# Memory and retention values projected 512 columns at a time, one token chunk to a PSUM bank

## The chip, the cores and the metric

The kernel runs on one core of a Trainium2 chip. The metric is the device time of one execution in microseconds (us), lower is better. The kernel before took 964.93 us (median of 3 runs, 964.29 to 968.08).

## What is computed

Two layers of a decoder trunk on 512 tokens of width 1024. Each layer normalizes the tokens, projects them with one combined matrix, runs four mixers on the parts, gates each, maps them back and adds the residual. Cut to the parts that matter here:

```python
hn = rmsnorm(x, pre_g)                       # (512, 1024)
proj = hn @ w_in                             # ret_q, ret_k, ret_v, ..., sb_q, sb_k, sb_v, mem_q, ...
k, v = split(rmsnorm(mem, mem_norm_g) @ w_mem_kv, 2)   # 256 memory tokens, k and v (256, 512)
y_mem = softmax(mem_q @ k.T * d**-0.5) @ v   # 4 heads of 128
y_sb  = stick_breaking(sb_q, sb_k, sb_v)     # 4 heads of 128, strictly causal
y_ret = retention(rope(ret_q), rope(ret_k), ret_v)     # 4 heads of 128, then a norm per head
y_ssd = ssd_mixer(xbc, z, dt, ...)
x = x + rmsnorm(concat(gated y's) @ w_out, post_g)
```

The values of the memory (256 tokens by 512 columns) and of the retention (512 tokens by 512 columns) are what the change touches.

## The kernel before

**Precision and matmuls.** Every operand is kept as a pair of tiles, a high part and a low part, and every product is three matmuls: high by high, high by low, low by high (`mm3`). The helper `mm` at L278 issues nearly all of them, so their rows all carry that line and are told apart by tiles: `pj` and `mx` are PSUM banks (a bank is 128 partitions by 512 float32), `hTh` and `hTl` the transposed normed tokens, `wh` and `wl` the weights, `s` and `y` working tiles. In the profile's names for a matmul, `pj<-wh,hTh` has the operand that streams first and the stationary one second.

**Weights.** They come from HBM in blocks of 1 MB (`raw`). Each block is two pieces of 128 x 1024, and each piece is split into `wh` (a cast on ACT, L286) and `wl` (a subtraction on DVE, L287). There are 5 buffers for pieces (`NSUB`) and 2 for blocks. A piece's buffer is free again when the last matmul that reads it is done, and only then can a later piece be split into it. For an "a" block a piece holds four 128-row chunks of the width by 256 columns.

**Projections with the tokens stationary.** `proj_a` computes 256 output columns for up to 4 token chunks of 128: two chunks share one PSUM bank, a piece is used for all chunks, and then the next piece follows. One call takes 2 pieces and 96 matmuls of 256 columns for 4 chunks, 48 for 2. `proj_b` has the weights stationary and 512 tokens streaming: one piece and 24 matmuls of 512 columns for 128 output features.

**PSUM.** There are two pools of 4 banks, `pj` and `mx`. A new bank can be taken when one of the four in its pool has been read for the last time.

**The order of the work.** In the first part of layer 0 (`start`) the instructions stand as written. After that a scheduler places the instructions of each engine at build time, and `tick` and `defer` decide after how many projections a later step of a head is issued. Each engine then works through its own fixed list, in that order, and waits where an operand or a bank is not ready.

**The stretch that matters here.** In a layer the stick-breaking heads run before the retention. Head h projects its query and its key (`proj_b` twice, into two `pj` banks). The query is read out by L531 (ACT) and L532 (DVE), the key by L286 (ACT) and L287 (DVE, `s<-pj`). Then follow, for each of four token blocks of 128, 256, 384 and 512 keys: the logits in an `mx` bank, an absolute value, an exponential and a logarithm on ACT (L619 and L255), then on DVE a maximum (L622), a running sum (L623) and a difference (L625), then an exponential (L255). `sb_head2` transposes the weights (L637) and splits them (L286 and L287, `s<-mx`), `sb_head3` multiplies them with the values into an `mx` bank. Those last steps of heads 2 and 3 are placed by the scheduler into the retention's value projection (`ret_v`) and the retention's first projections. `ret_v` itself calls `proj_a` twice (half 0 and half 1 of the columns, two banks each), reads each bank with a sum (L657), scales the sum (L658), and subtracts and scales it by four instructions, one for each chunk and head (L662), which is the last reading of the bank. Then it splits the result. `ret_head` goes on with `proj_b` for the query of retention head 0.

Of the kernel before, what the change touches and what calls it, by code (L numbers as in the profile page):

```python
# [16 lines left out]
P = 128  # L17
# [61 lines left out]
def pack_weights(w_in, w_mem_kv, w_out):  # L79
# [3 lines left out]
    for l in range(DEPTH):  # L83
        for kind, name, spec in BLOCKS:
            w = src[name][l]
            o = []
            for s in range(2):
                if kind == "b":
                    t = w[:, spec[s]:spec[s] + P].reshape(KC, P, P)
                elif kind == "o":  # L90
                    half, j = spec
                    rows = OUT_ROWS[4 * j + 2 * s:4 * j + 2 * s + 2]
                    t = np.stack([w[r:r + P, 512 * half:512 * half + 512] for r in rows])
                elif kind == "d":
# [73 lines left out]
class Builder:  # L168
# [196 lines left out]
    def proj_a(self, x=None, nt=NT, extra=0, between=(), turns=False):  # L365
# [154 lines left out]
    def mem_v2(self, b):  # L520
        nc, p = self.nc, Pair(self, 512, "y")
        for t in range(2):
            s, r = slice(256 * t, 256 * t + 256), self.mcol[:, t:t + 1]
            nc.scalar.activation(p.h[:, s], b[:, s], AF.Copy, scale=r)
            nc.vector.scalar_tensor_tensor(out=p.l[:, s], in0=b[:, s], scalar=r, in1=p.hf[:, s], op0=ALU.mult, op1=ALU.subtract)
        self.mv.append(p)


    def scaled_pair(self, b, scale):
# [49 lines left out]
    def mem_head3(self, h, pT, y):  # L579
        b = self.mx()  # L580
        for m in range(2):
            o = 256 * m + HD * (h % 2)
            v = self.mv[h // 2]
# [65 lines left out]
    def ret_v(self):  # L649

        nc = self.nc
        ginv = self.con("ginv", 16)
        out = [[None, None], [None, None]]
        for half in range(2):
            for i, b in enumerate(self.proj_a()):
                st = self.tiny(4)
                nc.vector.tensor_reduce(out=st, in_=v3(b, 4), op=ALU.add, axis=AX.X)  # L657
                nc.vector.tensor_scalar(out=st, in0=st, scalar1=-1.0 / HD, scalar2=None, op0=ALU.mult)  # L658
                vt = self.buf()
                for j in range(4):  # L660
                    t, h = 2 * i + j // 2, 2 * half + j % 2
                    nc.vector.tensor_scalar(out=vt[:, P * j:P * j + P], in0=b[:, P * j:P * j + P],  # L662
                                            scalar1=st[:, j:j + 1], scalar2=ginv[:, 4 * t + h:4 * t + h + 1],
                                            op0=ALU.add, op1=ALU.mult)
                out[i][half] = self.pair(vt)
        return out

    def rope(self, b):
# [42 lines left out]
    def ret_head2(self, h, v, sc, y):  # L711
        nc = self.nc
        b = self.mx()
        for c in range(NT):
            self.mm3(b[:, P * c:], *self.vcols(v, c, h), sc[c][0], sc[c][1], c == 0, c == NT - 1)
        nc.scalar.copy(y, b)
        sq = [self.buf(tag="r")[0:64] for _ in range(2)]
        for i in range(2):
# [227 lines left out]
    def out_proj(self, l):  # L946
# [51 lines left out]
        if not last:  # L998
            for i in range(2):
                self.mem_k2(self.mem_k(i))  # L1000
                self.behind(self.turn[i], self.last_mm)
            for i in range(2):
                self.mem_v()
            self.behind(self.turn[2], self.marks[1])

    def load_x(self, t):
        x = [self.buf(), self.buf()]
# [40 lines left out]
    def start(self):  # L1048
# [33 lines left out]
        hn.append(self.normed(xs[2], preB))  # L1082
        self.w_prefetch(6)
        self.w_load(4)
        v = [self.proj_a(self.mx_, 2, between=[lambda: self.turned(hn[1], 1)])[0]]
        hn.append(self.normed(xs[3], preB))
        self.w_prefetch(7)
        self.mem_add()
        v.append(self.proj_a(self.mx_, 2, between=[lambda: self.turned(hn[2], 2), self.mem_cols])[0])
        self.mem_row()  # L1090
        self.w_load(5)
        self.w_prefetch(10)
        self.turned(hn[3], 3)
        for i in range(2):
            self.mem_v2(v[i])
        self.w_prefetch(12)
        for i in range(2):
            self.mem_k2(k[i])
# [4 lines left out]

    def layer(self, l):
        self.exp_ln_phase()
        while len(self.mv) < 2:
            self.mem_v()
# [54 lines left out]
```

## Time and profile before

| | us |
|---|---|
| median of 3 runs | 964.93 (964.29 to 968.08) |
| the profiled execution | 965.41 |
| its span, first to last instruction | 963.5 |
| PE busy | 950.5 |
| DVE busy | 656.7 |
| ACT busy | 456.7 |
| POOL busy | 101.2 |

The granted TensorE clock was 0.999. Times in the rows are microseconds from the start of the span. Matmuls are pipelined and a matmul's shown duration includes its way through the array, so the pace of PE is read from the distance between the starts of neighbouring matmuls, and not from the duration of one. `[0.24 <-DVE s L532]` behind a row says that the engine stood idle for 0.24 us before it, and that this ended with the DVE instruction of line 532 that wrote a tile `s`.

### The profile page before, as it was taken

The numbers are of one execution on the slowest core, as the hardware profiler recorded it, in microseconds if no ns is written. First come the engines' busy times: TensorE is split into PE (matmuls) and PEld (weight loads), VectorE is DVE, ScalarE is ACT, GpSimd is POOL, SyncE is SP. The second block draws the span as 40 slices with busy tenths as digits, with TensorE's granted clock in tenths as the row PEclk, the third lists the DMA queues.
The fourth block names the chain that finished last, engine by engine and source line by source line (L and its number), as shares of the span: only waits on it lengthen the run. The fifth ranks groups of instructions, "written<-read, shape, count | busy, mean of one in ns | idle before, by whom it ended". The sixth has DMA issues, their size and how long they took to land.

```text
span 963.5 us, 13242 instructions
## 1 busy us (share of the span) xinstructions
PE 950.5 (99%) x5151; PEld 812.5 (84%) x5151; DVE 656.7 (68%) x1054; ACT 456.7 (47%) x842; POOL 101.2 (10%) x160
## 2 busy tenths in 40 slices
PE   8999999999999999999999999999999999999997
PEld 7998888988887878888899888898888878888886
DVE  5765567877877796864487464768776867867454
ACT  6543466534454343553455345765334543435341
POOL 1100000001231201100040000000002321102001
PEclk9999999999999999999999999999999999999999
DMA  9352212122232424253255221212123423323502
GB/s 344 113 176 88 88 45 79 53 88 88 66 132 99 142 103 129 86 188 142 90 185 193 93 88 53 80 45 88 60 79 95 140 99 121 108 101 121 189 30 87
DMA packets 26302, 105.79 MB, mean 110 GB/s; under 512 B 4096, under 2 KB 4352, under 8 KB 16896
## 3 DMA queue, kind: packets, MB, share of 16 engines
q10 hardware_dynamic: 10224, 73.44, 21.5%
q1 hardware_dynamic: 16016, 31.52, 10.0%
q8 instruction: 40, 0.66, 0.3%
q14 instruction: 22, 0.18, 0.1%
HBM read 100.63 MB, written 4.28 MB: 109 GB/s over the span
## 4 chain that ended last, share of the span: by engine, by line
PE 84%; DVE 6%; DMA 5%; ACT 2%; issue 1%; POOL 1%; SPq 0%; DVEq 0%; POOLq 0%; ACTq 0%
PE pj L278 61%; PE mx L278 21%; DMA s<-acs 1%; DVE wl L287 1%; DVE s L623 1%; DMA r<-row 1%; DVE s L786 1%; DMA raw<-wts 1%; PE mx L575 1%; DMA t<-r 1%; POOL t L687 1%; DMA mem<-memT 1%; PE mx L422 0%; DVE s L622 0%; ACT wh L286 0%
## 5 line engine op out<-in xcount | busy, mean ns | idle before, releaser
L278 PE MATMUL pj<-hTh,wh 128*128 128x512 f32 x704 | 277.6, 394 | 0.0
L278 PE MATMUL pj<-hTl,wh 128*128 128x512 f32 x704 | 276.6, 393 | 0.0
L278 PE MATMUL pj<-hTh,wl 128*128 128x512 f32 x704 | 275.4, 391 | 0.0
L287 DVE TENSOR_TENSOR wl<-raw,wh 128x1024 fp32r<-128x1024 f32 (+2 forms) x157 | 186.0, 1189 | 116.2 <-ACT wh L286 109.6
L286 ACT CAST wh<-raw 128x1024 fp32r<-128x1024 f32 (+2 forms) x157 | 160.1, 1023 | 180.1 <-PE pj L278 152.0
L278 PEld LDWEIGHTS pj<-hTh,wl 128*128 128x128 f32 x704 | 132.3, 188 | 26.7
L278 PEld LDWEIGHTS pj<-hTh,wh 128*128 128x128 f32 x704 | 132.3, 188 | 26.6 <-issue 0.2
L278 PEld LDWEIGHTS pj<-hTl,wh 128*128 128x128 f32 x704 | 132.4, 188 | 25.7
L278 PE MATMUL pj<-wh,s 128*128 128x512 f32 (+1 forms) x384 | 103.6, 355 | 0.0
L278 PE MATMUL mx<-s,s 128*128 128x256 f32 (+4 forms) x616 | 97.7, 310 | 0.3
L278 PEld LDWEIGHTS mx<-s,s 128*128 128x128 f32 (+1 forms) x616 | 84.7, 178 | 13.0 <-issue 3.1
L278 PE MATMUL mx<-wh,s 128*128 128x512 f32 x256 | 79.1, 389 | 0.0
L278 PEld LDWEIGHTS pj<-wh,s 128*128 128x128 f32 x384 | 68.3, 189 | 10.5
L278 PE MATMUL pj<-wl,s 128*128 128x512 f32 (+1 forms) x192 | 68.3, 356 | 1.4 <-DVE wl L287 1.4
L706 POOL TENSOR_SCALAR_AFFINE_SELECT s<-s 128x128 fp32r<-128x128 f32 x64 | 21.0, 361 | 417.6 <-DVE s L287 417.6
L278 PE MATMUL pj<-wh,hTh 128*128 128x256 f32 (+1 forms) x208 | 60.2, 290 | 0.5 <-DVE s L532 0.5
L287 DVE TENSOR_TENSOR s<-mx,s 128x512 fp32r<-128x512 f32 (+2 forms) x86 | 42.0, 515 | 26.1 <-ACT s L286 25.7
L278 PE MATMUL pj<-wl,hTh 128*128 128x256 f32 (+1 forms) x208 | 59.5, 286 | 0.0
L278 PE MATMUL pj<-wh,hTl 128*128 128x256 f32 (+1 forms) x208 | 58.5, 284 | 0.0
L278 PEld LDWEIGHTS mx<-wh,s 128*128 128x128 f32 x256 | 48.1, 188 | 10.0
L286 ACT CAST s<-mx 128x512 fp32r<-128x512 f32 (+2 forms) x86 | 36.7, 456 | 39.1 <-PE mx L278 23.1
L287 DVE TENSOR_TENSOR s<-y,s 128x512 fp32r<-128x512 f32 x64 | 41.2, 685 | 19.7 <-ACT s L286 14.0
(165 smaller groups left out, 1316.0 us busy)
## 6 DMA issues: line engine op xcount, KB each, us to landing
raw<-wts ACTq DMA_DIRECT2D x69, 1024.0 KB, 4.8
s<-x SPq DMA_DIRECT2D x24, 256.0 KB, 3.8
raw<-wts SPq DMA_DIRECT2D x4, 1024.0 KB, 8.6
s<-acs SPq DMA_DIRECT2D x16, 256.0 KB, 6.3
r<-row SPq DMA_DIRECT2D x12, 256.0 KB, 3.9
s<-acs SPq DMA_DIRECT2D x16, 128.0 KB, 6.3
x<-s SPq DMA_DIRECT2D x8, 256.0 KB, 2.0
out<-s SPq DMA_DIRECT2D x8, 256.0 KB, 2.0
```

The costliest lines, as they stand in the source:

```text
L278: return self.nc.tensor.matmul(out, lhsT, rhs, start=start, stop=stop)
L286: self.nc.scalar.copy(h, src)
L287: self.nc.vector.tensor_sub(l, src, hf)
L575: nc.tensor.transpose(b[:, P * t:P * t + P], w[t // 2][:, o:o + P], self.con("ident", P))
L623: nc.vector.tensor_tensor_scan(out=u[:, ::-1], data0=u[:, ::-1], data1=u[:, ::-1], initial=0.0, op0=ALU.add, op1=ALU.bypass)
L687: nc.gpsimd.tensor_tensor(out=c, in0=c, in1=self.mhalf[:RP], op=ALU.pow)
L706: nc.gpsimd.affine_select(out=d, in_=d, pattern=[[1, P]], compare_op=ALU.is_ge, fill=0.0, base=0, channel_multiplier=-1)
L786: nc.vector.scalar_tensor_tensor(out=acc[:, s:], in0=b[:, :SEQ - s], scalar=tap(3 - s), in1=acc[:, s:], op0=ALU.mult, op1=ALU.add)
```

## The change

Both value projections get 512 columns at once. A weight piece now holds two 128-row chunks of the width by 512 columns, so a projection takes four pieces, and a token chunk has a bank of its own that all four pieces add to. The retention's values fill four `pj` banks in place of two and two; the memory's fill two, one for each of its 256 tokens' chunks. A matmul has 512 columns in place of 256, and there are half as many. The readers follow: `ret_v` reads four banks of one token chunk and four heads each, and `mem_v2` two banks with one instruction for a chunk on ACT and one on DVE. The bytes of the weights and the number of pieces stay.

```diff
-    b += [("a", "w_mem_kv", GW + 256 * i) for i in range(2)]
+    b += [("v", "w_mem_kv", (GW, 512 * i)) for i in range(2)]
...
-    b += [("a", "w_in", RET_V + 256 * i) for i in range(2)]
+    b += [("v", "w_in", (RET_V, 512 * i)) for i in range(2)]
...
+    def proj_v(self, x=None, nt=NT, between={}):
+        self.tick(2)
+        xh, xl = x or self.hk
+        banks = [self.pj() for _ in range(nt)]
+        self.marks = []
+        for s in range(4):
+            if s == 2:
+                self.tick(2)
+            for f in between.get(s, ()):
+                f()
+            if self.starting:
+                self.w_prefetch(self.w_cur + 2)
+            wh, wl = self.w_take(2)
+            for t in range(nt):
+                ts = slice(P * t, P * t + P)
+                for j in range(2):
+                    kc = 2 * s + j
+                    self.mm3(banks[t], xh(kc)[:, ts], xl(kc)[:, ts], wh[:, j], wl[:, j], kc == 0, kc == KC - 1)
+                self.marks.append(self.last_mm)
+            self.w_prefetch()
+        return banks
...
     def mem_v(self):
-        self.mem_v2(self.proj_a(self.mx_, 2)[0])
+        self.mem_v2(self.proj_v(self.mx_, 2))
...
-        out = [[None, None], [None, None]]
-        for half in range(2):
-            for i, b in enumerate(self.proj_a()):
-                st = self.tiny(4)
-                nc.vector.tensor_reduce(out=st, in_=v3(b, 4), op=ALU.add, axis=AX.X)
-                nc.vector.tensor_scalar(out=st, in0=st, scalar1=-1.0 / HD, scalar2=None, op0=ALU.mult)
-                vt = self.buf()
-                for j in range(4):
-                    t, h = 2 * i + j // 2, 2 * half + j % 2
-                    nc.vector.tensor_scalar(out=vt[:, P * j:P * j + P], in0=b[:, P * j:P * j + P],
...
-                out[i][half] = self.pair(vt)
+        out = []
+        for t, b in enumerate(self.proj_v()):
+            st = self.tiny(HEADS)
+            nc.vector.tensor_reduce(out=st, in_=v3(b, HEADS), op=ALU.add, axis=AX.X)
+            nc.vector.tensor_scalar(out=st, in0=st, scalar1=-1.0 / HD, scalar2=None, op0=ALU.mult)
+            vt = self.buf()
+            for h in range(HEADS):
+                c = slice(HD * h, HD * h + HD)
+                nc.vector.tensor_scalar(out=vt[:, c], in0=b[:, c], scalar1=st[:, h:h + 1],
+                                        scalar2=ginv[:, 4 * t + h:4 * t + h + 1], op0=ALU.add, op1=ALU.mult)
+            out.append(self.pair(vt))
```

The scheduler's order changes with it, at three places of which each comes once in a layer. In the changed kernel's rows the lines have other numbers: L647, L648 and L650 are the former L622, L623 and L625; L558 is the former L532; L290 is L287; L681, L682 and L686 are L657, L658 and L662.

**DVE, middle of the value projection, layer 0.** `pj_1858` and `pj_1859` are the two banks of half 0, `pj_1682` and `pj_1731` hold query and key of stick-breaking head 3, `s_1604` belongs to head 2 and `s_1655` to `s_1659` to the transposed weights of head 1. Before:

```order
L622 SCALAR_TENSOR_TENSOR s_1604<-mx_1641,s_1604 128x512
L657 TENSOR_REDUCE t_1966<-pj_1858 128x4
L287 TENSOR_TENSOR s_1655<-mx_1660,s_1654 128x512
L623 SCALAR_TENSOR_TENSOR s_1604<-s_1604 128x512
L658 TENSOR_SCALAR t_1966<-t_1966 128x4
L287 TENSOR_TENSOR s_1657<-mx_1667,s_1656 128x384
L287 TENSOR_TENSOR s_1659<-mx_1673,s_1658 128x256
L532 SCALAR_TENSOR_TENSOR s_1714<-pj_1682,s_1713 128x512
L625 TENSOR_TENSOR s_1604<-mx_1641,s_1604 128x512
L657 TENSOR_REDUCE t_1978<-pj_1859 128x4
```

In the changed kernel `pj_1806` and `pj_1807` are the banks of token chunks 0 and 1, and `pj_1630` is the query's of head 3:

```order
L681 TENSOR_REDUCE t_1968<-pj_1806 128x4
L682 TENSOR_SCALAR t_1968<-t_1968 128x4
L681 TENSOR_REDUCE t_1980<-pj_1807 128x4
L647 SCALAR_TENSOR_TENSOR s_1552<-mx_1589,s_1552 128x512
L682 TENSOR_SCALAR t_1980<-t_1980 128x4
L290 TENSOR_TENSOR s_1603<-mx_1608,s_1602 128x512
L648 SCALAR_TENSOR_TENSOR s_1552<-s_1552 128x512
L290 TENSOR_TENSOR s_1605<-mx_1615,s_1604 128x384
L290 TENSOR_TENSOR s_1607<-mx_1621,s_1606 128x256
L650 TENSOR_TENSOR s_1552<-mx_1589,s_1552 128x512
L558 SCALAR_TENSOR_TENSOR s_1662<-pj_1630,s_1661 128x512
```

Both sums over the finished banks, and the difference for head 2, now stand ahead of the reading of head 3's query; before, one sum did.

**DVE, end of the value projection, layer 0.** Before, the first bank's last reading (L662 on `pj_1858`) stands ahead of the difference for head 3 (`s_1766`, 512 keys):

```order
L658 TENSOR_SCALAR t_2140<-t_2140 128x4
L623 SCALAR_TENSOR_TENSOR s_1766<-s_1766 128x512
L287 TENSOR_TENSOR s_1821<-mx_1835,s_1820 128x256
L662 TENSOR_SCALAR s_1969<-pj_1858,t_1966,consts 128x128 x4
L625 TENSOR_TENSOR s_1766<-mx_1803,s_1766 128x512
```

In the changed kernel the first bank's last reading (L686 on `pj_1806`) stands behind that difference (`s_1714`) and behind the splits of head 3's transposed weights (`s_1869` to `s_1873`):

```order
L290 TENSOR_TENSOR s_1767<-mx_1788,s_1766 128x128
L650 TENSOR_TENSOR s_1714<-mx_1751,s_1714 128x512
L290 TENSOR_TENSOR s_1869<-mx_1874,s_1868 128x512
L290 TENSOR_TENSOR s_1871<-mx_1881,s_1870 128x384
L290 TENSOR_TENSOR s_1871<-mx_1892,s_1870 128x128
L290 TENSOR_TENSOR s_1873<-mx_1887,s_1872 128x256
L686 TENSOR_SCALAR s_1971<-pj_1806,t_1968,consts 128x128 x4
```

The release of the first of the four value banks has moved past all the remaining work of head 3.

**PE, around the first matmul of the retention's query, layer 0.** Before, `pj_2164` is the query of retention head 0 and `mx_1996` the first transposes of head 3's weights:

```order
L278 MATMUL mx_1844<-s_1820,s_881 128x256
L278 MATMUL mx_1844<-s_1818,s_880 128x128
L637 MATMUL mx_1996<-consts,s_1764 128x128 x2
L637 MATMUL mx_1996<-consts,s_1765 128x128
L278 MATMUL pj_2164<-hTh,wh_1756 128x512
```

In the changed kernel `pj_2016` is that query, and `mx_1896` is the product of head 3's weights with the values, the last step of the stick-breaking heads:

```order
L281 MATMUL mx_1896<-s_1870,s_828 128x128
L281 MATMUL mx_1896<-s_1871,s_828 128x128
L281 MATMUL mx_1896<-s_1870,s_829 128x128
L281 MATMUL pj_2016<-hTh,wh_1704 128x512
L281 MATMUL pj_2016<-hTl,wh_1704 128x512
```

The rest of head 3, which stood among the matmuls of the retention's query and key, now stands ahead of them. Within the value projection PE takes chunk 0 and then chunk 1 through all four weight pieces, then head 3's first logits, then chunks 2 and 3.

More of the change, by code (lines that the diff above doesn't have):

```diff
@@ L93, in pack_weights @@
                     t = np.stack([w[r:r + P, 512 * half:512 * half + 512] for r in rows])
+                elif kind == "v":
+                    rows = slice(spec[1] + 256 * s, spec[1] + 256 * s + 256)
+                    t = w[rows, spec[0]:spec[0] + 512].reshape(2, P, 512)
                 elif kind == "d":
@@ L517, in mem_v, with mem_v2 @@
     def mem_v(self):
-        self.mem_v2(self.proj_a(self.mx_, 2)[0])
[L520 to L526, printed above, removed]
+        self.mem_v2(self.proj_v(self.mx_, 2))
+    def mem_v2(self, banks):
+        nc = self.nc
+        for t, b in enumerate(banks):
+            p, r = Pair(self, 512, "y"), self.mcol[:, t:t + 1]
+            nc.scalar.activation(p.h, b, AF.Copy, scale=r)
+            nc.vector.scalar_tensor_tensor(out=p.l, in0=b, scalar=r, in1=p.hf, op0=ALU.mult, op1=ALU.subtract)
+            self.mv.append(p)
     def scaled_pair(self, b, scale):
@@ L1001, in out_proj @@
                 self.behind(self.turn[i], self.last_mm)
-            for i in range(2):
-                self.mem_v()
-            self.behind(self.turn[2], self.marks[1])
+            self.mem_v()
+            self.behind(self.turn[2], self.marks[5])
     def load_x(self, t):
@@ L1084, in start, with v2 @@
         self.w_load(4)
[L1085 to L1089, printed above, removed]
+        def v2():
+            hn.append(self.normed(xs[3], preB))
+            self.w_prefetch(7)
+            self.mem_add()
+        v = self.proj_v(self.mx_, 2, between={1: [lambda: self.turned(hn[1], 1)], 2: [v2],
+                                             3: [lambda: self.turned(hn[2], 2), self.mem_cols]})
         self.mem_row()
@@ L1093, in start @@
         self.turned(hn[3], 3)
-        for i in range(2):
-            self.mem_v2(v[i])
+        self.mem_v2(v)
         self.w_prefetch(12)
```

10 lines of the change are left out of this document (3 added, 7 removed).

## The prediction

> **What bounds the kernel now.** I read the page's first rows, then the chain of work that ended last.
>
> ```profile
> span 963.5 us, 13242 instructions
> PE 950.5 (99%) x5151; PEld 812.5 (84%) x5151; DVE 656.7 (68%) x1054; ACT 456.7 (47%) x842; POOL 101.2 (10%) x160
> PE 84%; DVE 6%; DMA 5%; ACT 2%; issue 1%; POOL 1%; SPq 0%; DVEq 0%; POOLq 0%; ACTq 0%
> ```
>
> PE is busy almost throughout, and the chain lies on it for 84%. So a shorter list of matmuls shortens the run, if PE still finds work at each moment. That second half has to be read from the stretch of `ret_v`, by the busy time of each engine in it and by its first row on PE's timeline:
>
> ```profile
> 152.90:187.41 34.51, 34.40 (x272) 32.88 (x273) 25.55 (x49) 22.00 (x51) 0.00 (x0) 1.00 0.18 62
> 152.90 0.39 PE L278 MATMUL pj<-wh,hTh 128*128 128x256 f32 x1 [0.24 <-DVE s L532]
> ```
>
> The columns are PE, PEld, DVE, ACT, POOL, granted clock, DMA. DVE has 25.55 us of work in 34.51 us. It is the second engine here, and the value projection begins by waiting for it: the first matmul stood 0.24 us until L532 had read a `pj` bank. The clock is 1.00, so no pace below hides a throttle.
>
> **The matmuls, saved.** The pace of both shapes, from neighbouring starts on PE's timeline:
>
> ```profile
> 162.53 0.28 PE L278 MATMUL pj<-wh,hTh 128*128 128x256 f32 x1
> ...
> 163.61 0.29 PE L278 MATMUL pj<-wh,hTh 128*128 128x256 f32 x1
> 193.18 0.39 PE L278 MATMUL pj<-hTh,wh 128*128 128x512 f32 x1
> ...
> 197.03 0.39 PE L278 MATMUL pj<-hTh,wl 128*128 128x512 f32 x1
> ```
>
> Nine steps of 256 columns take 1.08 us, 0.120 each. Seventeen of 512 take 3.85 us, 0.2265 each. Two narrow ones cost 0.240, one wide one 0.2265, so each removed matmul saves 13.5 ns. Per layer 96 go in `ret_v` (192 become 96) and 48 in the memory's values (96 become 48). That is 1.3 us and 0.65 us, over two layers **3.9 us**, if PE never waits instead.
>
> The Trainium skill, "TensorE: Matmul & The Clock Gate", section "Back-to-back issue gap", gives an isolated gap of N/2.4 + 2.5 ns. By it two halves would cost only 2.5 ns more than one whole, and 288 fewer matmuls would save 0.7 us; the forecast would be 3.2 us higher. The trace does not agree (120 and 226.5 ns against 109 and 216), and the measurement decides.
>
> **The middle of `ret_v`, added wait A.** All four `pj` banks are now open at once. Banks 0 and 1 are there at the start, but chunk 2 needs the one that holds the query of stick-breaking head 3, which L532 frees. DVE's and PE's timelines before:
>
> ```profile
> 163.74 0.60 PE L637 MATMUL mx<-consts,s 128*128 128x128 f32 x4
> 164.09 0.36 PE L278 MATMUL pj<-wl,hTh 128*128 128x256 f32 x1
> 168.18 0.27 PE L637 MATMUL mx<-consts,s 128*128 128x128 f32 x1
> 168.56 1.92 PE L278 MATMUL mx<-s,s 128*128 128x512 f32 x10
> 170.32 0.33 PE L278 MATMUL pj<-wh,hTh 128*128 128x256 f32 x1
> 165.58 0.68 DVE L657 TENSOR_REDUCE t<-pj 128x4 f32<-128x512 f32 x1
> 166.18 0.68 DVE L287 TENSOR_TENSOR s<-mx,s 128x512 fp32r<-128x512 f32 x1
> 166.78 1.21 DVE L623 TENSOR_TENSOR_SCAN s<-s 128x512 f32<-128x512 f32 x1
> 167.91 0.14 DVE L658 TENSOR_SCALAR t<-t 128x4 f32<-128x4 f32 x1
> 167.96 0.88 DVE L287 TENSOR_TENSOR s<-mx,s 128x384 fp32r<-128x384 f32 x2
> 168.76 0.68 DVE L532 SCALAR_TENSOR_TENSOR s<-pj,s 128x512 fp32r<-128x512 f32 x1
> 169.36 0.68 DVE L625 TENSOR_TENSOR s<-mx,s 128x512 f32<-128x512 f32 x1
> 169.96 0.68 DVE L657 TENSOR_REDUCE t<-pj 128x4 f32<-128x512 f32 x1
> ```
>
> Distances of starts give what each occupies DVE: 0.60 for a 512-wide step and for the sum, 1.13 for the running sum, 0.05 for L658, 0.80 for the two narrower splits. Before, L532 stood ahead of the second sum, which can only run when PE has finished that bank. In the new order it stands behind it. So from the moment PE ends chunk 1, DVE has: second sum 0.60, L622 0.60, L658 0.05, split 0.60, running sum 1.13, splits 0.80, L625 0.60, L532 0.68, together 5.1 us. PE meanwhile has head 1's ten transposes (four took 0.35, so 0.9) and ten matmuls of its product (168.56 to 170.32, 1.76) and two first logits (0.2), 2.8 us. The product cannot run ahead, since it needs those splits. **Wait A is 5.1 - 2.8 = 2.3 us.** The stretch before had about 0.3 us of this kind (168.18 to 168.56).
>
> Least: if the second sum and L622 are done as PE ends chunk 1 (1.2 us of the list), 1.1. Most: if two more 512-wide steps lie ahead of them, 3.5. I take the sum of the rows.
>
> **The end of `ret_v`, added wait B.** Retention's query needs a fifth `pj` bank, and all four hold values. The first is free after L662. Before, this stood ahead of head 3's last steps; now it stands behind them all. Rows of DVE and ACT with the durations for that list:
>
> ```profile
> 174.15 0.75 ACT L619 ACTIVATE s<-mx 128x128 f32<-128x128 f32 x2 [3.44 <-PE mx L278]
> 175.63 0.73 DVE L622 SCALAR_TENSOR_TENSOR s<-mx,s 128x128 f32<-128x128 f32 x2 [2.99 <-ACT s L255]
> 176.27 1.00 DVE L623 TENSOR_TENSOR_SCAN s<-s 128x128 f32<-128x128 f32 x2
> 177.19 0.60 DVE L625 TENSOR_TENSOR s<-mx,s 128x128 f32<-128x128 f32 x2
> 178.25 0.56 DVE L622 SCALAR_TENSOR_TENSOR s<-mx,s 128x384 f32<-128x384 f32 x1 [0.46 <-ACT s L255]
> 178.84 0.96 DVE L623 TENSOR_TENSOR_SCAN s<-s 128x384 f32<-128x384 f32 x1
> 179.71 1.20 DVE L287 TENSOR_TENSOR wl<-raw,wh 128x1024 fp32r<-128x1024 f32 x1
> 180.83 0.55 DVE L625 TENSOR_TENSOR s<-mx,s 128x384 f32<-128x384 f32 x1
> 185.71 1.36 DVE L662 TENSOR_SCALAR s<-pj,t,consts 128x128 f32<-128x128 f32 x4
> 187.58 0.28 DVE L287 TENSOR_TENSOR s<-mx,s 128x128 fp32r<-128x128 f32 x1
> 170.07 0.63 ACT L255 ACTIVATE s<-s 128x512 f32<-128x512 f32 x1 [0.48 <-DVE s L625]
> 180.96 0.57 ACT L286 CAST s<-mx 128x512 fp32r<-128x512 f32 x1
> ```
>
> From head 3's first L622 to the first L662 the new DVE list holds: its 128 and 256 blocks 0.64 + 0.92 + 0.60; its 384 block 0.59 + 0.87 + 0.55; four weight splits at 1.12, 4.48, all in this stretch because chunks 2 and 3 hold the pieces to the end; two sums and two L658, 1.3; the 512 block 0.60 + 1.13 + 0.60; head 2's transposed splits 0.60 + 0.80 + 0.20. That is 13.9 us. Then L255 on ACT (0.63), a transpose group (0.35), the copy (0.57) and the hand-overs, 1.7 us in which DVE has nothing; then head 3's splits 1.6 and L662 1.36. **18.6 us.** It starts after chunk 2's first 17 matmuls (3.85), about 0.9 us of logits, and 1.5 us of ACT (174.15 to 175.63), 6.2 us after chunk 2 began. So the bank is free 24.8 us after that.
>
> PE's own work in that time: 48 matmuls of chunks 2 and 3, 10.9; the rest of head 3's logits, about 2.0 (as a product of ten, 1.76, and the small ones); two groups of ten transposes, 1.8; two products of twelve, 3.8; together 18.5 us. **Wait B is 24.8 - 18.5 = 6.3 us.** It cannot be filled: what PE had there before, the retention's query and key, is what waits. The work behind the waiting matmul is everything that remains of the layer. Least: if only the 5.3 us pass between chunk 2 and head 3's L622 that passed before (170.32 to 175.63), 5.4. Most: if each of some four small waits within costs another 0.4 us of hand-over, 8.
>
> **Per layer** 2.3 + 6.3 - 1.3 - 0.3 = 7.0 us, twice, **14.0 us**.
>
> **The memory's values.** At the start two matmul groups already wait for weight splits:
>
> ```profile
> 23.64 0.39 PE L278 MATMUL pj<-wl,s 128*128 128x256 f32 x1 [0.88 <-DVE wl L287]
> 28.16 0.39 PE L278 MATMUL pj<-wl,s 128*128 128x256 f32 x1 [0.50 <-DVE wl L287]
> ```
>
> The second is the second value piece; a first piece that ends 0.16 us sooner only waits longer. So I count 0.3 to 0.65 us there and 0.65 us in layer 1, where the projection lies between `w_out` matmuls, together **1.1 us saved**. `mem_v2` with half as many instructions, and the slices that `mem_head3` reads, cost nothing: they lie behind some 23 us of `sb_v` matmuls; without that cover four instructions of 512 columns would be at most 2.5 us. The DMA's bytes, blocks and queue places are the same.
>
> **Sum.** 14.0 - 1.1 = +12.9 us. The profiled execution took 965.41 us (span 963.5), 0.5 us over the median 964.93, so 978.3 by its own time and 977.8 by the median. I say **978.0**.
>
> **The rivals.**
> - *The banks come free in time.* Place: the first matmul of the retention's query. If DVE's 18.6 us were covered by PE's work, only the 3.9 us of matmuls would remain: 961.1 us, 0.4% faster. It decides at a list shorter than PE's 12.3 us that are left when it starts. For it: DVE is busy only 74% of the stretch (25.55 of 34.51). Against: its free time lies where it waits for ACT and PE, ahead of this list, not in it. The Trainium skill, "Perfetto Trace Analysis", section "Matmuls", says that larger matmuls are more efficient where possible, and this would be its outcome. The same section asks that groups rotate through banks so that reading one overlaps the next group's matmuls; 0.24 us at 152.90 shows the trace agreeing. Chance 0.09.
> - *Half the wait.* If DVE and ACT run head 3's chain ahead of its place in my count, or if the stall at A lets DVE catch up so that B shrinks, each layer pays 2 to 4 us net: 967.5 to 972. Chance 0.16.
> - *Weights late.* The fourth split needs a block whose DMA is issued only when an older block's second split is done, and its copy stands on ACT ahead of head 3's copies. Two groups of the page's DMA issues, the last column the time to landing:
>
> ```profile
> raw<-wts ACTq DMA_DIRECT2D x69, 1024.0 KB, 4.8
> raw<-wts SPq DMA_DIRECT2D x4, 1024.0 KB, 8.6
> ```
>
> Should it land as late as the slower group, ACT and so the bank come 8.6 - 4.8 = 3.8 us later in each layer, 985.6. Against: seven ACT instructions stand between issue and copy, some 4 us, so that at 4.8 little is missing. Chance 0.07.
>
> **How the numbers follow.** The forecast (973 to 983) has 0.68. From the bounds: least 1.1 + 5.4 - 1.6 = 4.9 per layer, 974; most 3.5 + 8 - 1.6 = 9.9, 984. The half wait reaches down to 967.5; with it the range is 967.5 to 984, and the first rival and the third are left out. What a measurement of this kernel tells from no change is about 0.5%, 4.8 us: faster means under 960.1, slower over 969.8. Faster: a third of the first rival, 0.03. Same: the rest of it and a third of the second, 0.11. Slower: 0.86.
>
> **What would show it.** PE's timeline after: 512-column `pj<-wh,hTh` matmuls at 0.2265 us (matmul term). Two idle spells of PE in each layer, ended by DVE: one of 2 to 3 us between chunks 1 and 2, ended by L532's or L287's successors; one of some 6 us in parts ahead of the first `pj<-hTh,wh` behind the values, ended by splits of `s<-mx` and by L686. PE busy 3 to 5 us lower, DVE's the same. I am wrong if these spells are absent, if the sum of PE's new idle time is under 8 us, or if waits elsewhere (the start, the `r` rows) make the difference.

## The result, and the profile after

The changed kernel takes 978.49 us (median of 4 runs, 977.50 to 979.65), against 964.80 us for the kernel before in the same comparison: a ratio of 1.0137 over the single runs (the two medians alone give 1.0142), 95% interval 1.0124 to 1.0150. It is slower by 13.7 us. The profiled execution took 977.50 us, with a span of 975.6; it is the shortest of the four, so the two profiles lie 12.1 us apart and not 13.7. From here on lines have the changed kernel's numbers, 3 or more above those of before: `mm` is L281, the split L286/L287 is L289/L290, L637 is L662, L657 and L658 are L681 and L682, L662 is L686.

The page's first rows after:

```profile
span 975.6 us, 12655 instructions
PE 953.9 (98%) x4863; PEld 801.8 (82%) x4863; DVE 655.2 (67%) x1050; ACT 456.9 (47%) x838; POOL 99.6 (10%) x160
```

There are 288 matmuls fewer, yet PE's busy time is 3.4 us higher; why is seen below. PE's idle time went from 13.0 us (963.5 less 950.5) to 21.7. Cut into stages, from the first matmul of a retention's value projection to the first of the retention's query, and from there to the first of `w_out`, the busy time of the engines (columns PE, PEld, DVE, ACT, POOL, granted clock, DMA) shows where. Before, layers 0 and 1, without the row already shown:

```profile
187.41:398.46 211.05, 209.64 (x1032) 173.91 (x1031) 161.03 (x246) 88.60 (x138) 33.61 (x50) 1.00 0.30 100
398.46:511.64 113.18, 113.18 (x604) 97.86 (x602) 70.95 (x97) 58.70 (x105) 17.10 (x26) 1.00 0.45 155
624.86:659.37 34.51, 34.40 (x273) 32.88 (x273) 25.57 (x49) 22.00 (x51) 0.00 (x0) 1.00 0.17 62
659.37:869.71 210.34, 209.24 (x1032) 173.87 (x1031) 161.20 (x246) 88.61 (x138) 33.43 (x50) 1.00 0.30 100
```

And after:

```profile
153.11:198.15 45.04, 39.45 (x197) 31.98 (x197) 29.51 (x57) 24.48 (x57) 0.00 (x0) 0.96 0.13 47
198.15:403.84 205.69, 205.69 (x1008) 171.48 (x1009) 157.01 (x237) 86.67 (x132) 32.77 (x50) 1.00 0.31 102
403.84:516.54 112.70, 112.70 (x555) 95.24 (x554) 70.53 (x97) 59.45 (x106) 17.32 (x26) 1.00 0.45 154
629.75:676.24 46.49, 40.87 (x198) 33.31 (x198) 29.51 (x57) 24.39 (x57) 0.00 (x0) 0.93 0.13 45
676.24:881.89 205.65, 205.65 (x1009) 171.46 (x1009) 156.77 (x237) 86.58 (x132) 32.78 (x50) 1.00 0.31 102
```

The stage of the values got 10.53 and 11.98 us longer, the one behind it 5.36 and 4.69 shorter, since the last steps of head 3 now stand ahead of the query; the `w_out` stage of layer 0, with the memory's values, got 0.48 shorter. That is all of the 12.1 us between the spans but 0.1. Within the first of these stages PE's timeline, without the value projection's own rows:

```profile
166.89 1.15 PE L662 MATMUL mx<-consts,s 128*128 128x128 f32 x9
169.10 0.33 PE L662 MATMUL mx<-consts,s 128*128 128x128 f32 x1 [1.06 <-DVE s L290]
170.68 2.19 PE L281 MATMUL mx<-s,s 128*128 128x512 f32 x12 [1.25 <-DVE s L290]
172.71 0.40 PE L281 MATMUL pj<-wh,hTh 128*128 128x512 f32 x1
...
186.43 0.49 PE L662 MATMUL mx<-consts,s 128*128 128x128 f32 x3
187.68 0.41 PE L662 MATMUL mx<-consts,s 128*128 128x128 f32 x2 [0.77 <-DVE t L682]
188.86 0.33 PE L662 MATMUL mx<-consts,s 128*128 128x128 f32 x1 [0.77 <-DVE s L290]
189.92 3.48 PE L281 MATMUL mx<-s,s 128*128 128x512 f32 x10 [0.73 <-DVE s L290]
193.20 0.62 PE L662 MATMUL mx<-consts,s 128*128 128x128 f32 x3
193.58 0.42 PE L281 MATMUL mx<-s,s 128*128 128x128 f32 x2
193.83 1.17 PE L662 MATMUL mx<-consts,s 128*128 128x128 f32 x7
195.88 2.14 PE L281 MATMUL mx<-s,s 128*128 128x512 f32 x12 [0.88 <-DVE s L290]
198.15 0.50 PE L281 MATMUL pj<-hTh,wh 128*128 128x512 f32 x1
```

Wait A is the idle time up to 172.71, where chunk 2 begins; wait B the idle time in parts up to 198.15, where the query begins. DVE's own rows show what B ends with:

```profile
179.50 0.29 DVE L647 SCALAR_TENSOR_TENSOR s<-mx,s 128x128 f32<-128x128 f32 x1 [6.55 <-ACT s L258]
...
192.63 0.69 DVE L650 TENSOR_TENSOR s<-mx,s 128x512 f32<-128x512 f32 x1
195.14 1.69 DVE L290 TENSOR_TENSOR s<-mx,s 128x512 fp32r<-128x512 f32 x4 [1.82 <-ACT s L289]
196.74 1.36 DVE L686 TENSOR_SCALAR s<-pj,t,consts 128x128 f32<-128x128 f32 x4
```

The first bank is free at 198.10, and the query starts 0.05 us later. But little of B is a wait for that bank alone. The last product of twelve starts at 195.88 and, as the equal one at 170.68 shows, PE needs 2.03 us for it, so PE is through with the head at 197.91, and only the last 0.24 us can be the bank's. The rest of B stands ahead of the head's own transposes and products.

One row above is odd: the ten matmuls at 189.92 take 3.28 us to the next row's start, 1.76 before. The granted clock, microsecond by microsecond (the last figure but two):

```profile
190.00:191.00 1.00, 1.00 (x3) 0.81 (x4) 1.00 (x2) 0.00 (x0) 0.00 (x0) 0.51 0.99 418
191.00:192.00 1.00, 1.00 (x5) 0.90 (x4) 1.00 (x1) 0.00 (x0) 0.00 (x0) 0.50 0.18 74
192.00:193.00 1.00, 1.00 (x5) 0.77 (x4) 1.00 (x5) 0.00 (x0) 0.00 (x0) 0.50 0.00 0
193.00:194.00 1.00, 1.00 (x10) 1.00 (x10) 0.32 (x1) 0.63 (x1) 0.00 (x0) 0.78 0.00 0
```

PE ran at half its clock for some 3.4 us behind the idle spell. That also lifts its busy time.

### The profile page after: what moved, and what is told of

Read it like the earlier page. It is cut to its first block, busy times and chain, and to the rows that moved or that the text cites. A ratio compares the mean times of both kernels' runs of the same rounds, so it can differ in the third digit from the quotient of the medians.

```text
span 975.6 us, 12655 instructions
## 1 busy us (share of the span) xinstructions
PE 953.9 (98%) x4863; PEld 801.8 (82%) x4863; DVE 655.2 (67%) x1050; ACT 456.9 (47%) x838; POOL 99.6 (10%) x160
## 4 chain that ended last, share of the span: by engine, by line
PE 89%; DVE 5%; ACT 2%; DMA 1%; issue 1%; POOL 0%; DVEq 0%; SPq 0%; POOLq 0%; ACTq 0%
PE pj L281 66%; PE mx L281 22%; DVE wl L290 1%; DVE s L648 1%; DVE s L290 1%; DMA raw<-wts 1%; PE mx L601 1%; DVE s L647 1%; DMA mem<-memT 1%; ACT s L258 1%; PE mx L448 0%; ACT wh L289 0%; DVE s L650 0%; PE mx L871 0%; ACT s L491 0%
## 5 line engine op out<-in xcount | busy, mean ns | idle before, releaser
L290 DVE TENSOR_TENSOR wl<-raw,wh 128x1024 fp32r<-128x1024 f32 (+2 forms) x157 | 187.2, 1195 | 136.2 <-ACT wh L289 129.8
L281 PE MATMUL pj<-hTh,wh 128*128 128x512 f32 x704 | 276.6, 393 | 0.3
L281 PE MATMUL pj<-hTl,wh 128*128 128x512 f32 x704 | 276.5, 393 | 0.0
L281 PE MATMUL pj<-hTh,wl 128*128 128x512 f32 x704 | 275.6, 391 | 0.0
L289 ACT CAST wh<-raw 128x1024 fp32r<-128x1024 f32 (+2 forms) x157 | 160.6, 1026 | 206.5 <-PE pj L281 174.4
L281 PEld LDWEIGHTS pj<-hTh,wh 128*128 128x128 f32 x704 | 132.3, 188 | 27.2 <-DVE s L686 0.5
L281 PEld LDWEIGHTS pj<-hTh,wl 128*128 128x128 f32 x704 | 132.3, 188 | 27.0
L281 PEld LDWEIGHTS pj<-hTl,wh 128*128 128x128 f32 x704 | 132.4, 188 | 26.0
L281 PE MATMUL mx<-s,s 128*128 128x256 f32 (+4 forms) x616 | 101.3, 320 | 5.8 <-DVE s L290 5.8
L281 PEld LDWEIGHTS mx<-s,s 128*128 128x128 f32 (+1 forms) x616 | 88.3, 185 | 19.4 <-DVE s L290 7.3
L281 PE MATMUL pj<-wh,s 128*128 128x512 f32 x320 | 100.3, 391 | 0.1
L281 PE MATMUL mx<-wh,s 128*128 128x512 f32 x256 | 79.1, 389 | 0.0
L281 PEld LDWEIGHTS pj<-wh,s 128*128 128x128 f32 x320 | 59.9, 188 | 12.9 <-ACT wh L289 0.3
L281 PE MATMUL pj<-wl,s 128*128 128x512 f32 x160 | 62.5, 391 | 1.4 <-DVE wl L290 1.4
L281 PEld LDWEIGHTS mx<-wh,s 128*128 128x128 f32 x256 | 48.1, 188 | 9.9
L290 DVE TENSOR_TENSOR s<-mx,s 128x512 fp32r<-128x512 f32 (+2 forms) x86 | 41.7, 517 | 20.5 <-ACT s L289 20.5
L290 DVE TENSOR_TENSOR s<-y,s 128x512 fp32r<-128x512 f32 x64 | 41.3, 687 | 19.7 <-ACT s L289 14.0
L289 ACT CAST s<-mx 128x512 fp32r<-128x512 f32 (+2 forms) x86 | 35.7, 459 | 32.3 <-PE mx L281 23.8
L289 ACT CAST s<-y 128x512 fp32r<-128x512 f32 x64 | 36.6, 620 | 30.0 <-PE mx L281 22.0
L258 ACT ACTIVATE s<-s 128x128 f32<-128x128 f32 (+3 forms) x96 | 41.4, 468 | 19.2 <-DVE s L650 18.3
L281 PE MATMUL mx<-wl,s 128*128 128x512 f32 x128 | 49.6, 389 | 0.0
```

The lines of the kernel that those rows point to most:

```text
L258: i = self.nc.scalar.activation(out, in_, func, **k)
L281: return self.nc.tensor.matmul(out, lhsT, rhs, start=start, stop=stop)
L289: self.nc.scalar.copy(h, src)
L290: self.nc.vector.tensor_sub(l, src, hf)
```

## Experiments

**Each part alone.** `mem_wide` has the wide projection for the memory only, `ret_wide` for the retention only:

```diff
     b += [("v", "w_mem_kv", (GW, 512 * i)) for i in range(2)]
-    b += [("v", "w_in", (RET_V, 512 * i)) for i in range(2)]
+    b += [("a", "w_in", RET_V + 256 * i) for i in range(2)]      # mem_wide; ret_wide the other way round
```

> Only the memory's values are projected 512 columns at a time; the retention's values are as before. Theory (the loss is all in the retention's values): 96 matmuls fewer at 13.5 ns, at the start hidden in part behind weight splits, so 0.95 to 1.3 us under the kernel before, about 963.7 us at its 964.8, and the waits of PE around 150 to 200 us as before. Rival (the memory's values cost something, at the start or among the w_out matmuls of layer 0): 966 us or more, with a new idle spell of PE before 60 us or between 400 and 500 us.

> Only the retention's values are projected 512 columns at a time; the memory's are as before. Theory: the whole loss is here, so 1.1 us above the changed kernel, about 979.6 us, ratio 1.0153, with both idle spells of PE in each layer. Rival (the two projections disturb one another, by buffers or by a shifted order): 976 us or less.

`ret_wide` took 979.06 us, ratio 1.0141 (1.0126 to 1.0157): all of the loss is in the retention. `mem_wide` took 967.65, ratio 1.0027 (1.0015 to 1.0038): my theory missed by 4 us. The time is the rival's, its place is not. Its value stages are the 34.51 us of before, and its `w_out` stage is the 112.70 of the changed kernel, as expected. The time went in layer 1, in a place that the change does not touch. PE's and DVE's rows of `mem_wide`:

```profile
784.55 0.59 PE L281 MATMUL mx<-r,onesr 128*1 128x512 f32 x1 [3.60 <-DVE r L748]
784.93 0.63 PE L281 MATMUL pj<-hTh,wl 128*128 128x512 f32 x1
785.36 0.63 PE L281 MATMUL pj<-hTh,wh 128*128 128x512 f32 x1
781.23 0.69 DVE L758 TENSOR_TENSOR y<-y,r 128x512 f32<-128x512 f32 x1 [8.13 <-DMA r<-row]
```

DVE stood 8.13 us at L758 (L757 in the changed kernel, L733 before), which needs a row that goes through memory by DMA; the next head's variance (L748, or L747 and L723) stands behind it, and PE behind that. The clock is halved after it (0.43 us between starts in place of 0.2265). In the kernel before the same wait is 1.0 to 1.1 us in both layers. The row's 2 KB write, issued at 774.1 in `mem_wide`, landed after 4.0 us while a weight block was arriving; before, issued at 773.5, after 1.3. So `mem_wide_pool` takes L758 off DVE:

```diff
-        self.nc.vector.tensor_mul(y, y, rB)
+        self.nc.gpsimd.tensor_mul(y, y, rB)
```

> mem_wide, with the retention's last scaling of a head (L758, y times the broadcast row r) moved from DVE to POOL, so that DVE no longer stands still until that row's DMA has landed. Theory (mem_wide lost its time in layer 1 by a row that landed late, 4.0 us for 2 KB in place of 1.3, at which DVE waited 8.1 us and PE behind it 3.6 us, with a slow clock after it): that wait of PE goes, 962 to 964 us. Rival (the loss has another cause): 966.5 us or more.

It took 961.32 us, ratio 0.9957 (0.9941 to 0.9972), 6.3 us less and 0.7 under the range of the theory, and PE has no wait there in either layer. That DVE's standing at L758 made the loss is shown (the gain is larger than the loss, since the shorter wait of the kernel before goes too); that the weight block delayed the row is only read from when both moved.

**What wait B hangs on.** `halves` reads the first two banks out ahead of chunks 2 and 3; `pool_split` takes the low parts of four weight pieces off DVE; `no_ticks` issues no step of a head within the projection. The three edits in short:

```diff
+        for half in range(2):                          # halves: within proj_v
+            banks = [self.pj() for _ in range(2)]      # then all four pieces for chunks 2*half, 2*half+1
...
+            yield from banks
...
-        self.nc.vector.tensor_sub(l, src, hf)          # pool_split: pieces split within ret_v
+        self.nc.gpsimd.tensor_sub(l, src, hf)
...
-        self.tick(2)                                   # no_ticks: both in proj_v
+        self.tick(0)
```

> The changed kernel, but the retention's values of token chunks 0 and 1 go through all four weight pieces and are read out by DVE before chunks 2 and 3 are asked for; the matmuls stay 512 columns wide. Theory (in wait B the retention's query lacks a pj bank, since the readers of the first banks stand behind all of the last stick-breaking head's work): the first banks are free before that work, the query fills part of B, and 2 to 4 us are saved, 974.5 to 976.5 us. Rival (PE waits in B for the head's own transposes and mx banks, and the query would not fill it): 978 to 980 us.

> The changed kernel, but the low parts of the weight pieces that are split inside the retention's value projection are subtracted on POOL in place of DVE (four pieces in a layer, 4.5 us of DVE's list by the rows of before). Theory (wait B is DVE's list between chunk 2 and the first bank): the list gets up to 4.5 us shorter and B with it, by 2 to 4.5 us in each layer, so 969.5 to 974.5 us. Rival (what PE waits for in B is the turnover of mx banks between transposes and their splits, with ACT in the loop, and not DVE's amount of work): 977 to 980 us.

> The changed kernel, but no later step of a stick-breaking head is issued inside the value projection: the last steps of heads 2 and 3 come four units later, beside the retention's queries and keys. Theory (B arises where these steps meet a value projection that holds all four pj banks): B and its slow clock go, A stays with 2.8 us in each layer, and what the steps disturb in the retention's heads costs 1 to 3 us per layer, so 968 to 973 us. Rival (the steps cost the same wherever they are): 977 us or more.

`halves` took 978.48 us, ratio 1.0142 (1.0128 to 1.0156), as long as the changed kernel and so the time of the rival, though its query begins at 194.39, 3.8 us sooner. The stage behind gives it all back:

```profile
153.44:194.39 40.95, 36.36 (x180) 29.52 (x181) 27.27 (x53) 21.83 (x50) 0.00 (x0) 0.96 0.14 52
194.39:404.36 209.97, 208.56 (x1029) 173.65 (x1027) 158.73 (x242) 88.61 (x138) 34.09 (x50) 1.00 0.30 100
```

PE's idle time in both together is 6.0 us, against 5.6 in the changed kernel: 1.0 less in the values, 1.4 more behind, where the wait for a head's variance (L747 in the changed kernel, L723 before) has come back. The rest of the longer stage is the head's last work, which now stands behind the query. An earlier bank alone gains nothing.

`pool_split` took 979.81 us, ratio 1.0152 (1.0139 to 1.0166): the rival. The list from L647 to L686 is no shorter, 20.0 us against 18.6, with 4.5 us of DVE's work gone. Its rows on DVE (line numbers one higher than in the changed kernel):

```profile
184.30 2.07 DVE L649 TENSOR_TENSOR_SCAN s<-s 128x384 f32<-128x384 f32 x1
198.42 1.68 DVE L291 TENSOR_TENSOR s<-mx,s 128x512 fp32r<-128x512 f32 x4 [4.83 <-ACT s L290]
```

The freed time was not won, and DVE's busy time in the stage fell by 1.9 us only (29.51 to 27.58): the 384-wide running sum took 2.07 us beside POOL's subtractions (0.95 in the changed kernel), the 512 block still waited for ACT (0.16 us), and at the end DVE stood 4.83 us while PE, at half clock from 191 to 198 us, went through the product and the transposes. Layer 0 has more time at half clock here than the changed kernel's (6.8 us in B and 3.4 behind A, against 3.4), so layer 1 is the fairer comparison, with one spell of 3.4 us in B:

```profile
633.00:678.02 45.02, 39.04 (x198) 31.88 (x198) 26.96 (x53) 23.95 (x57) 10.18 (x4) 0.96 0.14 47
```

That is as long as the 45.04 us of the changed kernel's layer 0, which also has one spell, and the list took 19.9 us there too, with DVE waiting 2.58 and 2.99 us for ACT. B is a loop over ACT, DVE and PE, of which DVE's list is the longest part but not the only one.

`no_ticks` took 975.37 us, ratio 1.0104 (1.0089 to 1.0118), 3 us less, but not within the 968 to 973 of the theory. Only its profiled execution, at 972.42 us the shortest of four, lies there; the others took 975.2 to 975.9. In that profile B and the slow clock are gone and A stays, as the theory says: the value stage takes 33.57 us with 2.3 idle. The stage behind is longer than in the kernels above, with 3.1 us idle:

```profile
152.60:186.17 33.57, 31.25 (x161) 25.69 (x161) 19.89 (x40) 19.26 (x45) 0.00 (x0) 1.00 0.09 32
186.17:401.00 214.83, 211.74 (x1049) 176.40 (x1048) 165.68 (x255) 90.91 (x143) 32.74 (x50) 1.00 0.30 103
```

**The slow clock.** `keep_busy` gives PE something to do in the idle spells:

```diff
+            if (h, j) in ((1, 2), (1, 3), (2, 1), (2, 2), (2, 3), (3, 3)):
+                c = min(P * j, 2 * P)
+                for _ in range(3 * 2 * P // c):
+                    self.mm(b[:, 0:c], self.b16[:, 0:P], self.b16[:, 0:c], True, True)
             self.split(b[:, P * j:], *wT[j])
```

> The changed kernel with short bf16 matmuls of zero use (256 or 128 columns, three to six in a place) behind six transpose groups of stick-breaking heads 1, 2 and 3, where PE idles; they write parts of banks that nobody reads, and change nothing else. Theory of the clock: in the changed kernel PE's granted clock falls to 0.50 for about 3.4 us after three idle spells (from 190 us, from 647 us and from 668 us), which makes products that take 1.8 to 2.0 us last 3.3 to 3.6 us; if idleness is the cause, these spells are gone or rarer and the time falls by 1.5 us for each, to about 974 us. Rival (the clock does not depend on PE's idleness there, or the lost time was wait anyway): 978 to 980 us and the clock still at 0.50 in these places.

It took 978.58 us (1.0127 to 1.0154), as the changed kernel, but its clock did change: of the three spells at 0.50 only the one from 667 us is left in its profile, and the mean granted clock of its four executions is 0.993 to 0.996, against 0.989 to 0.993. Its rows of layer 0, for the place shown above and the whole stage:

```profile
192.00:193.00 1.00, 1.00 (x7) 0.77 (x6) 1.00 (x4) 0.00 (x0) 0.00 (x0) 1.00 0.00 0
153.36:198.32 44.96, 40.15 (x218) 32.25 (x218) 29.50 (x57) 24.26 (x57) 0.00 (x0) 1.00 0.14 48
629.90:675.85 45.95, 41.19 (x218) 33.51 (x219) 29.50 (x57) 24.35 (x57) 0.00 (x0) 0.96 0.14 46
```

So work in the idle spells takes most of the slow clock away, which speaks for idleness as its cause, and the time is the rival's. The comparison is not quite clean: the scheduler moved one split of DVE behind the running sum, and the ten matmuls start 38.0 us into layer 0's stage in place of 36.8. What ends B in layer 0 is DVE's L650, done 40.2 us into the stage in both kernels (193.32 in the changed one); the product is over before it, slow or fast, and the stage takes 44.96 us against 45.04. So there a slow product only fills a wait. In layer 1 A's spell went, which had made that stage 1.45 us longer than layer 0's. But the spell that stayed holds the product until 671.0, 0.9 us behind L650, and DVE stands 2.70 us for it in place of 1.70, so 0.54 us are won.

**The same matmuls in another place.** `early_wide` projects the retention's values ahead of stick-breaking head 3; `early_wide1` is the same with the units counted otherwise:

```diff
-        ysb = [self.sb_head(h, v) for h in range(HEADS)]
-        v = self.ret_v()
+        ysb = [self.sb_head(h, v) for h in range(3)]
+        vr = self.ret_v()
+        ysb += [self.sb_head(h, v) for h in range(3, HEADS)]
+        v = vr
...
-        self.defer(3, self.sb_head2, h, v, w, y)
+        self.defer(5, self.sb_head2, h, v, w, y)       # early_wide1: 4
...
-        self.tick(2)                                   # in proj_v, first and second
+        self.tick(0)                                   # early_wide1: 1, then 0
```

`early_narrow`, `early_narrow1` and `early_all_narrow` have the same order with the retention's values 256 wide (`proj_a`, its units set as there), the last with the memory's too.

> As no_ticks, but the retention's values are projected ahead of stick-breaking head 3, and the transposes of the weights of a head come five units after it in place of three, so that the value projection finds no transposes and products of a head around it. Theory (the width itself is cheap, and only its place between the heads' last steps costs): neither A nor B is left, the matmuls saved show, 961 to 964 us. Rival (a projection that holds four banks makes PE wait wherever it is): 967 us or more.

> As early_wide in place and order, with the retention's values projected 256 columns at a time as before (the memory's stay 512 wide). Theory (in a good place each removed matmul saves its 13.5 ns): 192 more matmuls than early_wide, so 2.6 us slower than it. Rival (the place makes the gain, and the four banks of the wide one still cost as much as its matmuls save): as fast as early_wide within 0.5 us, or faster.

> As early_wide, with one unit counted at the start of the value projection and a head's transposes four units after it in place of five, so that the last steps of head 3 no longer fall on the scores of retention head 0, where early_wide waited 1.68 us in each layer. Theory (every removed matmul saves its 13.5 ns wherever PE finds work): 2.6 us under early_narrow's 959.7, so 957.1 us, and no idle spell of PE behind 60 us. Rival (four held banks cost at least as much as their matmuls save in any place): 959.5 us or more.

> early_wide1 with the retention's values 256 columns wide, all counts of units as there. Theory: 2.6 us over early_wide1 and level with early_narrow, 959.7 us. Rival (the one unit made the gain of early_wide1): within 0.7 us of early_wide1.

> early_narrow with the memory's values 256 columns wide too, so that nothing of the change is left but the new place and order. Theory (the memory's values save 0.65 us in layer 1 and 0.3 to 0.65 us at the start, when no chance wait hides it): 0.95 to 1.3 us over early_narrow, 960.7 to 961.0 us. Rival (the memory's wide values cost, as mem_wide's 2.8 us suggest): below 959.5 us.

| kernel | us, median | ratio to before, 95% |
|---|---|---|
| `early_wide` | 961.83 | 0.9968 (0.9956 to 0.9981) |
| `early_narrow` | 959.73 | 0.9953 (0.9939 to 0.9967) |
| `early_wide1` | 959.75 | 0.9939 (0.9924 to 0.9953) |
| `early_narrow1` | 960.29 | 0.9946 (0.9933 to 0.9958) |
| `early_all_narrow` | 960.48 | 0.9945 (0.9933 to 0.9958) |

The first two and the other three were measured against different series of runs of before (964.80 and 965.65 us), so the ratios are compared. `early_wide1` has the lowest ratio, and all five beat both kernels. The place makes the gain: `early_all_narrow`, with every projection as narrow as before, is 0.55% faster than the kernel before. In its profile the waits for L532, L723 and L789 (3.0 us in the two layers before) are gone; where the rest of its 5 us comes from was not traced. What the width adds is in the stages, here of `early_wide` and then of `early_narrow`:

```profile
134.94:163.60 28.66, 28.66 (x142) 23.47 (x141) 21.99 (x39) 19.02 (x42) 0.00 (x0) 1.00 0.10 37
163.60:396.27 232.67, 230.99 (x1156) 192.89 (x1155) 176.91 (x277) 103.79 (x172) 32.68 (x50) 1.00 0.30 99
134.90:164.91 30.01, 30.01 (x241) 28.72 (x239) 26.86 (x50) 19.79 (x44) 0.00 (x0) 1.00 0.14 44
164.91:395.35 230.44, 230.44 (x1154) 192.56 (x1152) 172.44 (x266) 103.02 (x170) 32.74 (x50) 1.00 0.30 99
```

The wide values take 1.35 us less, two short transposes of head 3 among it that the narrow kernel has ahead of its query. But the wide kernel waits 1.68 us later in each layer, for head 3's last split, and ends up slower. In `early_wide1` that wait is gone. Its two stages of layer 1, and then those of `early_narrow1`:

```profile
604.43:633.62 29.19, 29.19 (x145) 23.75 (x144) 21.00 (x41) 18.25 (x42) 0.00 (x0) 1.00 0.00 1
633.62:863.76 230.14, 230.14 (x1151) 192.31 (x1150) 180.05 (x275) 104.97 (x172) 35.61 (x50) 1.00 0.31 105
604.87:637.84 32.97, 32.97 (x262) 31.55 (x261) 28.48 (x54) 21.58 (x48) 0.00 (x0) 1.00 0.15 56
637.84:865.25 227.41, 227.41 (x1132) 189.63 (x1131) 172.92 (x262) 100.94 (x166) 35.70 (x50) 1.00 0.29 98
```

Together they take 259.33 us against 260.38, with no idle time in either: 1.05 us for 96 matmuls, 11 ns each. In the whole time the two cannot be told apart: 0.9939 and 0.9946 lie well within each other's intervals, since a wait for a head's variance of 0.8 and 1.7 us in layer 0 and a start that differs by 1.5 us (to the first value projection, 135.98 against 134.50) lie over them. Of the expectations, that of `early_wide` held for the time, though a wait came that it did not have; the 2.6 us between wide and narrow retention did not show in the time, where the rivals of `early_narrow`, `early_wide1` (959.75, not 957.1) and `early_narrow1` held; and `early_all_narrow` at 960.48, between its theory and its rival, shows nothing of the memory's term either, which is 0.48 us in its `w_out` stage (113.18 against 112.70).

## Why the prediction was right

The forecast was 978.0 us, and 978.49 came. The mechanism held: two new waits of PE in each layer, at the places named, ended by DVE. That the number is 0.5 us off is partly luck, since several errors of 1 to 4 us stand against each other. By its own steps:

- **The matmuls saved**, 13.5 ns each: about 11 in the pair `early_wide1` and `early_narrow1`, so 1.05 us per layer in place of 1.3. The Trainium skill, "TensorE: Matmul & The Clock Gate", section "Back-to-back issue gap", gives a formula by which, as an estimate, 96 matmuls would have saved 0.24 us; the trace speaks for the larger figure.
- **Wait A**, 2.3 us: the brackets of its two rows make 2.31, but with the draining of PE's pipeline ahead of each, by the starts, it is about 2.9 (5.82 us from 166.89 to 172.71, less 2.03 for the product and 0.9 for ten transposes). What is waited for is DVE's splits of head 1. The step let A end with L532, now L558, and set the product against the whole list. But the product needs the splits, which are 3.8 us into the step's own list, and 2.03 us of product behind them end at 5.8, later than L558 at 5.1. L558 indeed ends half a microsecond before chunk 2 starts.
- **Wait B**, 6.3 us: DVE's list was put at 18.6 us, and it is 18.60 (179.50 to 198.10). It begins 6.8 us after chunk 2 in place of 6.2, and PE's own work was 19.2 us in place of 18.5; these two cancel. From 186.43 to 198.15, 11.7 us, PE has 16 transposes (1.4) and two products of twelve (2.03 each), at full clock 5.5, so 6.2 are lost, 1.5 of them as slow clock in place of idleness. The size held; the cause that the step gave it did not quite. It put all on the bank that the query lacks, which PE waits for 0.24 us. `halves` gave the query its bank 3.8 us sooner and won nothing, and `pool_split` cut DVE's list without shortening it in time. The wait belongs to the heads' last steps, which meet a stretch in which PE has no other work; `early_all_narrow`, with a new place for the projection and later transposes, shows that this cost some 5 us before the change too. Why the wide projection makes it so much dearer in the old place than the narrow one is read from the new order of the lists; no run keeps the old order with the wide matmuls.
- **Together per layer.** By the stages: layer 0's values grew by 10.53 us. The stage behind lost 24 matmuls that moved ahead, by the distances of starts about 3.1 us (an estimate: a product of twelve, ten transposes and two short ones). So 10.53 - 3.1 + 1.3 = 8.7 us of waiting came in, which is about A's 2.9 and B's 6.2 less the 0.3 of before, and 11.98 - 3.1 + 1.3 = 10.2 in layer 1, against 8.6 - 0.3 = 8.3 in the sum.
- **Left out of the sum**: first, the slow clock behind A in layer 1, at 647 us, 1.45 us; the same product in layer 0 ran at full clock. Second, a credit: the stage behind shrank by 5.36 and 4.69 us, 2.3 and 1.6 more than the work that moved. Of that 1.41 and 1.10 us are idle time of PE before, mainly for L723; in the changed kernel PE waits for nothing there, probably because it is late by then, as `halves` suggests, where the wait is back. The layers lost 5.17 and 7.29 us net, 12.5 together, against 14.0.
- **The memory's values**, -1.1: the `w_out` stage gained 0.48 us in every kernel with wide memory values, in place of 0.65. At the start no gain can be seen; the two waits for weight splits there are 0.77 and 0.62 us, 0.88 and 0.50 before. That the order of a kernel can pay 4 us for it elsewhere, by a row that lands late, `mem_wide` showed; the sum had no term for that.
- **The tests named**: the two spells per layer are there, with 8.7 us of new idle time in the whole kernel, little over the 8 that were asked. A's brackets end with splits, as said; B's are 3.15 us in layer 0 and end with splits and L682, none with L686. The test on PE's busy time failed (3.4 us higher, not 3 to 5 lower); matmuls at half clock count longer, and so, by the shown durations, does one after a wait. Late weights, the third rival, do not show: behind 60 us PE waits for no weight split in either kernel.

## What to carry to other kernels

Fewer, wider matmuls saved about 11 ns each here, and a single new wait of 1.7 us per layer eats what 96 of them save. Before widening a projection so that it holds every bank of a pool, look at what else is under way on the other engines, and move it to where no chain is: here the place, with the order that goes with it, was worth 5 us and the width at most 2.6. When a wait is removed, look behind it for the one that comes back.

## Of the hardware, not expected

An idle spell can cost twice. After some 3 us with little on PE (3.1 us to 190.0, 27% busy) the granted clock fell to 0.50 and stayed there for about 3.4 us. Longer spells were about two and three times that: 6.8 us in layer 0 of `pool_split`, and 10.2 us in both layers of one run of `ret_wide`, with PE busy in part. From its layer 0:

```profile
192.00:195.00 3.00, 2.45 (x11) 2.03 (x10) 2.60 (x6) 0.36 (x1) 0.00 (x0) 0.53 0.14 57
195.00:198.00 3.00, 2.24 (x12) 1.84 (x10) 0.79 (x2) 2.27 (x6) 0.00 (x0) 0.50 0.00 0
198.00:201.00 3.00, 3.00 (x10) 2.71 (x10) 2.17 (x7) 0.00 (x1) 0.00 (x0) 0.50 0.02 5
```

That execution took 984.24 us, others of the same kernel 978.2 to 982.1. The same spell A brought it in layer 1 and not in layer 0 of one execution. The Trainium skill, "TensorE: Matmul & The Clock Gate", section "What's actually happening", has two clocks, full and half, set by a window of some 3.4 us that runs on its own; the figures here agree, and a window that runs on its own would fit that one of two equal spells brings it; no run here tries that.
